# Compact 64x64 operands for the two heads of a pair, in two quarters of TensorE (RWKV core and attention)

## The chip, the cores and the metric

The kernel runs on one core of a Trainium2 chip. The metric is the device time of one execution in microseconds (us), the median of several runs.

## What is computed

Two layers of an encoder over 256 tokens of width 1024, in float32. Each layer has a token mixer with four groups (attention, bidirectional RWKV-7, pooling, gated convolution) and a channel mixer (dense in layer 0, eight experts in layer 1). The change touches the RWKV group (4 heads of 64, in two directions) and the attention group (4 heads of 64).

```python
def rwkv7_step(S, inp):
    r, w, k, v, a_vec, b_vec = inp
    sa = jnp.einsum('...ij,...j->...i', S, a_vec)
    S = S * w[..., None, :] + sa[..., :, None] * b_vec[..., None, :] + v[..., :, None] * k[..., None, :]
    return S, jnp.einsum('...ij,...j->...i', S, r)
...
    xs = (to_time(r), to_time(decay), to_time(k), to_time(v), to_time(-kk), to_time(kk * a))
    S0 = jnp.zeros((2, bsz, H, N, N), jnp.float32)
    _, ys = lax.scan(rwkv7_step, S0, xs)
    ys = jnp.moveaxis(ys, 0, 2)
    y = ys[0] + jnp.flip(ys[1], axis=1)
...
    y_a = neighbourhood_attention(za[..., :G], za[..., G:2 * G], za[..., 2 * G:], rpb)
    y_b = rwkv7_bidirectional(zr, lg, mu, w0, w2, a0, a2, k_k, k_a, r_k, lnx_w, lnx_b, g2)
    y_c = multiscale_pool(zp, pool_w, pool_scale)
    y_d = short_gated_conv(zc, conv_w)
    return jnp.concatenate([y_a, y_b, y_c, y_d], axis=-1) @ w_out
```

## The kernel before

The program runs `mixer(0)`, `ffn_layer(0)`, `mixer(1)` and `moe_layer(1)` one after the other. Weights come in chunks of 1 MB through a ring of three `raw` tiles on SyncE's queue (`raw_chunk`, L208); `chunk` splits each into two float32r parts, `whi` on ScalarE (L220) and `wlo` on VectorE (L221), and a projection is three matmuls per block (L173 to L175).

The RWKV scan is done in four chunks of 64 tokens per direction, for two heads at a time. `rw_prep(hp)` prepares the operands of pair `hp`; `rw_core(hp)` does the scan. A tile holds the channels of the two heads one above the other, head 0 in partitions 0 to 63 and head 1 in 64 to 127. So that one 128x128 matmul serves both heads, `bd4` and `put_bd` (L381, L387) lay each operand out as a block-diagonal 128x128 matrix per chunk, zeros in the off-diagonal blocks (names bdA, bdB, bdK, bdV). All 128x128 intermediates, `X`, `XT`, `nT`, `P1`, `Ub`, `Sb`, have that form and are 512 columns wide for four chunks.

The steps of a core, with `e` for the two directions and four chunks `c` each:

- `s1` (bdB with `ar`, 128 moving columns) and `s3` (bdA with bdB) start `X` and `nT` (L544 to L557).
- Five levels invert a triangular matrix: VectorE transposes `X` into `XT` (L563), `p1` multiplies `nT` and `X`, ScalarE copies the result to `P1` (L568), `p2` multiplies `XT` and `P1`, VectorE copies it into `X` under a mask (L574). Between levels stand `s2` (bdK with `ar`, L582 to L584) and the transposes `sk` of V, B and K (L593, L595).
- The recurrence over four chunks: `sV` with `ak`, `Sb` with bdA, a copy `tU` (L610), `X` with `tU`, a copy `Ub` (L612), then `sK` and `sB` products and the new state `Sb` (L623, L625).
- The outputs `y`: for each head a sum of up to six products of 128x64 stationary columns, in the column half of that head.

Every part of the mixer is a generator: "z" the projections for RWKV, "q" and "r" `rw_prep(0)` and `rw_prep(1)`, "0" and "1" the two cores, "a" attention, "p" pooling, "c" convolution, "f" fillers (chunks of the conditioning weights, a product and sum of 128x1024 on VectorE, L257), "g" a row, "o" the output projections (matmuls named ya). The string `ORDER[l]` says which part makes its next step; a scheduler then sets the order on each engine, so projections (z, ya) stand between the steps of the cores. `psum` has two rings of four banks; a core takes its banks from one of them (`bk`).

Attention computes the scores of two heads as two matmuls of 128 rows against the same `kt`, with a query tile `qz` whose other half is zero (L713), into one bank; the values `pv` are computed for 128 columns of which 64 are used.

## Time and profile before

| | us |
|---|---|
| median of 3 runs (lowest, highest) | 1547.24 (1546.98, 1551.23) |
| the profiled execution | 1546.37 |
| its span, first to last instruction | 1544.5 |
| TensorE busy | 1443.1 (93%) |
| VectorE busy | 645.8 (42%) |
| ScalarE busy | 435.5 (28%) |
| GpSimd busy | 24.9 (2%) |

Busy shares are means over stages with different limits, so the sections below go by stage and by start times. A float32 matmul appears as two records of TensorE. A record's duration is the latency of one; records are pipelined, and their pace is the distance between starts.

### The profile page before, as it was taken

To read this page: it belongs to the slowest core of one execution; us is meant where nothing else is said; L and a number is where in the kernel's file an instruction comes from. 1 tells how busy PE (TensorE), PEld (TensorE's weight loads), DVE (VectorE), ACT (ScalarE), POOL (GpSimd) and SP (SyncE) were. 2 spreads that over 40 slices of the span, in tenths; PEclk is the share of its full clock that TensorE was granted. 3 is DMA by queue.
4 is the path that set the end of the run, shared out by engine and by line. 5 is a ranking of instruction groups with operands and counts; after the bars stand their busy time and mean duration, and the time that the engine had idled before them with its cause. 6 is when DMAs were issued, how large, how long until landed. Compare 5 with 4: busy or idle time off the path is not lost. (4 is left out here: it accounts for less than half of the span.)

```text
span 1544.5 us, 28342 instructions
## 1 busy us (share of the span) xinstructions
PE 1443.1 (93%) x12174; PEld 875.5 (57%) x12174; DVE 645.8 (42%) x1194; ACT 435.5 (28%) x814; POOL 24.9 (2%) x91
## 2 busy tenths in 40 slices
PE   3999989999998999989889899999999999998885
PEld 2988979999997999963223233433433234332222
DVE  7799869977856777651010021020020110110202
ACT  4854645544437746350011000010010010000101
POOL 1001000000001001000000000000000000000000
PEclk9999999999999999999999999999999999999998
DMA  9556138987743411189999999999999999999995
GB/s 373 215 204 227 55 146 340 394 339 306 293 158 122 158 55 42 45 323 363 416 415 416 417 417 417 416 415 382 412 417 416 417 415 416 416 415 416 416 410 194
DMA packets 85253, 487.79 MB, mean 316 GB/s; under 512 B 9841, under 2 KB 10225, under 8 KB 40946
## 3 DMA queue, kind: packets, MB, share of 16 engines
q1 hardware_dynamic: 83522, 482.98, 78.3%
q10 hardware_dynamic: 1584, 2.68, 0.6%
q8 instruction: 113, 1.85, 0.5%
q14 instruction: 34, 0.28, 0.0%
HBM read 484.57 MB, written 1.05 MB: 314 GB/s over the span
## 5 line engine op out<-in xcount | busy, mean ns | idle before, releaser
L170 PE MATMUL u<-mw,xe 128*32 128x512 f32 (+1 forms) x3368 | 359.0, 537 | 20.1 <-DMA mw<-in_moe_dram 18.7
L1179 DVE TENSOR_TENSOR sg<-sg,u 128x256 f32<-128x256 f32 (+1 forms) x96 | 34.3, 380 | 650.6 <-ACT sg L1178 650.6
L170 PEld LDWEIGHTS u<-mw,xe 128*32 128x32 f32 x3368 | 114.5, 109 | 220.8 <-issue 160.4
L1178 ACT ACTIVATE sg<-u 128x256 f32<-128x256 f32 (+1 forms) x96 | 30.8, 355 | 666.0 <-PE u L170 656.5
L170 PE MATMUL y<-mw,sT 128*32 128x512 f32 x1480 | 180.4, 594 | 15.5 <-DMA mw<-in_moe_dram 10.8
L221 DVE TENSOR_TENSOR wlo<-raw,whi 128x1024 fp32r<-128x1024 f32 x142 | 169.8, 1218 | 46.7 <-ACT whi L220 46.5
L220 ACT ACTIVATE whi<-raw 128x1024 fp32r<-128x1024 f32 x142 | 146.4, 1056 | 137.1 <-issue 43.6
L170 PE MATMUL u<-mwhi,xe 128*32 128x512 f32 (+1 forms) x748 | 172.6, 551 | 0.4 <-PEq L1132 0.3
L170 PE MATMUL u<-mwlo,xe 128*32 128x512 f32 (+1 forms) x748 | 150.7, 551 | 0.5 <-PEq L1132 0.2
L174 PE MATMUL g<-hlo,whi 128*128 128x256 f32 x448 | 126.9, 284 | 0.5 <-DVE hlo L339 0.3
L173 PE MATMUL g<-hhi,whi 128*128 128x256 f32 x448 | 126.9, 284 | 0.0
L175 PE MATMUL g<-hhi,wlo 128*128 128x256 f32 x448 | 126.6, 283 | 0.0
L170 PEld LDWEIGHTS y<-mw,sT 128*32 128x32 f32 x1480 | 52.5, 109 | 128.0 <-issue 84.7
L257 DVE CUSTOM_DVE_ANT_0 raw<-raw,row,pcs 128x1024 f32<-128x1024 f32 x96 | 120.3, 1278 | 4.5 <-ACT row L1362 3.9
L170 PE MATMUL y<-mwhi,sT 128*32 128x512 f32 x324 | 96.2, 594 | 0.1
L173 PE MATMUL z<-hhi,whi 128*128 128x256 f32 x304 | 88.9, 293 | 4.1 <-ACT whi L220 4.0
L170 PEld LDWEIGHTS u<-mwhi,xe 128*32 128x32 f32 x748 | 46.2, 109 | 79.7 <-issue 70.0
L175 PE MATMUL z<-hhi,wlo 128*128 128x256 f32 x304 | 88.1, 290 | 2.2 <-DVE wlo L221 2.2
L174 PE MATMUL z<-hlo,whi 128*128 128x256 f32 x304 | 87.6, 289 | 0.5 <-DVE hlo L339 0.3
L174 PEld LDWEIGHTS g<-hlo,whi 128*128 128x128 f32 x448 | 85.9, 192 | 1.6 <-DVE hlo L339 1.2
L173 PEld LDWEIGHTS g<-hhi,whi 128*128 128x128 f32 x448 | 86.0, 192 | 0.6
L175 PEld LDWEIGHTS g<-hhi,wlo 128*128 128x128 f32 x448 | 85.9, 192 | 0.0
(317 smaller groups left out, 2022.8 us busy)
## 6 DMA issues: line engine op xcount, KB each, us to landing
mw<-in_moe_dram SPq DMA_DIRECT2D x232, 1024.0 KB, 15.0
mwlo<-in_moe_dram SPq DMA_DIRECT2D x104, 512.0 KB, 12.6
mwhi<-in_moe_dram SPq DMA_DIRECT2D x104, 512.0 KB, 13.8
raw<-in_ada_dram SPq DMA_DIRECT2D x44, 1024.0 KB, 6.7
raw<-in_ffn_dram SPq DMA_DIRECT2D x42, 1024.0 KB, 7.1
raw<-in_win_dram SPq DMA_DIRECT2D x20, 1024.0 KB, 4.9
raw<-in_wout_dram SPq DMA_DIRECT2D x6, 1024.0 KB, 5.0
raw<-in_ada_dram SPq DMA_DIRECT2D x8, 512.0 KB, 7.1
```

What stands on the lines that cost most here:

```text
L170: pe.matmul(o, a, b, start=start, stop=stop)
L173: pe.matmul(o, ah, bh, start=start, stop=False)
L174: pe.matmul(o, ah, bl, start=False, stop=False)
L175: pe.matmul(o, al, bh, start=False, stop=stop)
L220: ops[0].append(act.activation(hi, raw[:, c], AF.Copy))
L221: ops[1].append(dve.tensor_sub(lo, raw[:, c], hi.bitcast(F32)))
L257: r = dve.tensor_tensor_reduce(w, w, cB, scale=1.0, scalar=P(l, "ab", v * KB + k), op0=OP.mult, op1=OP.add, accum_out=mods[l][:, v, k:k + 1])
L1178: other_set(act.activation(sg, u[:, 0:w], AF.Silu))
L1179: dve.tensor_mul(sg, sg, u[:, w:2 * w])
```

## The change

Block-diagonal operands are gone. `mmh` makes each product as two 64x64 matmuls, one per head: rows 0 to 63 into partitions 0 to 63 of the bank, rows 64 to 127 into partitions 64 to 127. Every tile of the core that was 512 columns wide for four chunks becomes 256 wide (`half`, a ring of 38; the wide ring goes from 47 to 36), and masks, `tU` and `sd` are half as wide. `rw_prep` hands `bc`, `kf`, `zv` and `ar` on as they are, without the 16 copies and 16 fills per pair. The transposes `sk` become products with a 64x64 identity. `y` alternates the heads product by product. In attention the query tile is compact, each head's scores are a matmul over 64 rows into a bank of its own, two additions of 256 columns take the place of one of 512, and `pv` computes 64 columns. The first half of the last output projection becomes a part of its own, "O", behind the other parts; `ORDER` is unchanged.

```diff
...
-NSLOT = 47
+NSLOT = 36
+NHALF = 38
...
-            def bd4(name):
-                b = slot_(name).rearrange("p (n h t) -> p n h t", n=4, h=2)
-                pool.memset(b[0:64, :, 1, :], 0.0)
-                pool.memset(b[64:128, :, 0, :], 0.0)
-                return b
-
-            def flat(b, n):
-                return b[:, n].rearrange("p h t -> p (h t)")
+            def half(name):
+                return mp.tile([128, 256], F32, name=name, tag="h", bufs=NHALF).rearrange("p (n f) -> p n f", n=4)
 
             HS = [slice(0, 64), slice(64, 128)]
 
-            def put_bd(b, src):
-                for h in range(2):
-                    act.activation(b[HS[h], :, h, :], src[HS[h]], AF.Copy)
+            def mmh(o, a, b, start=True, stop=True):
+
+                for h in HS:
+                    mm(o[h], a[h], b[h], start, stop)
...
                 zv = zmix(4 + hp, "zdv")
-                B = {n: [] for n in "ABKV"}
-                for e in range(2):
-                    for n, src in (("B", c4(bc)[:, e]), ("A", ar[e][:, :, 0, :]), ("K", c4(kf)[:, e]),
-                                   ("V", c4(zv)[:, e])):
-                        b = bd4("bd" + n)
-                        put_bd(b, src)
-                        B[n].append(b)
-                    yield
-                st_r[hp] = dict(eP=eP, ar=ar, bc=c4(bc), B=B)
+                st_r[hp] = dict(eP=eP, ar=ar, B=c4(bc), K=c4(kf), V=c4(zv))
+                yield
...
                 for e in range(2):
-                    X[e] = v4(slot_("X"))
-                    act.activation(X[e], ident[:, None, :].to_broadcast([128, 4, 128]), AF.Copy)
+                    X[e] = half("X")
+                    act.activation(X[e], b4(C("i2")[:, None, :]), AF.Copy)
                     p = bk[hp]("s1").rearrange("p (c m t) -> p c m t", c=4, m=2)
                     for c in range(4):
-                        mm(p[:, c], flat(B["B"][e], c), ar[e][:, c])
-                    dve.copy_predicated(X[e].rearrange("p n (h t) -> p n h t", h=2),
-                                        b4(mx[:, 0, e].rearrange("p (h t) -> p h t", h=2)[:, None]),
-                                        p[:, :, 0:1, :].to_broadcast([128, 4, 2, 64]))
+                        mmh(p[:, c], R["B"][:, e, c], ar[e][:, c])
+                    dve.copy_predicated(X[e], b4(mx[:, 0, e, None, :]), p[:, :, 0, :])
                     dve.tensor_mul(arb[:, 4 * e:4 * e + 4, :], p[:, :, 1, :], b4(m1i[:, e, None, :]))
-                    p = v4(bk[hp]("s3"))
+                    p = pq("s3")
                     for c in range(4):
-                        mm(p[:, c], flat(B["A"][e], c), flat(B["B"][e], c))
-                    nT[e] = v4(slot_("nT"))
+                        mmh(p[:, c], ar[e][:, c, 0], R["B"][:, e, c])
+                    nT[e] = half("nT")
                     dve.tensor_mul(nT[e], p, b4(m3[:, e, None, :]))
-                    XT[e] = v4(slot_("XT"))
+                    XT[e] = half("XT")
...
                 for lv in range(NLV):
-                    pt = [None, None]
                     P1 = [None, None]
                     for e in range(2):
                         dve.transpose(XT[e], X[e])
-                        pt[e] = v4(bk[hp]("p1"))
+                        p = pq("p1")
                         for c in range(4):
-                            mm(pt[e][:, c], nT[e][:, c], X[e][:, c])
-                        P1[e] = v4(slot_("P1"))
-                        act.activation(P1[e], pt[e], AF.Copy)
+                            mmh(p[:, c], nT[e][:, c], X[e][:, c])
+                        P1[e] = half("P1")
+                        act.activation(P1[e], p, AF.Copy)
                         yield
                     for e in range(2):
-                        p = v4(bk[hp]("p2"))
+                        p = pq("p2")
                         for c in range(4):
-                            mm(p[:, c], XT[e][:, c], P1[e][:, c])
+                            mmh(p[:, c], XT[e][:, c], P1[e][:, c])
                         dve.copy_predicated(X[e], b4(mx[:, lv + 1, e, None, :]), p)
...
-                                mm(p[:, c], flat(B["K"][e], c), ar[e][:, c])
+                                mmh(p[:, c], R["K"][:, e, c], ar[e][:, c])
                             dve.tensor_mul(ark[:, 4 * e:4 * e + 4, :], p[:, :, 1, :], b4(m1i[:, e, None, :]))
-                            ak[e] = v4(slot_("ak"))
-                            dve.tensor_mul(ak[e].rearrange("p n (h t) -> p n h t", h=2),
-                                           p[:, :, 0:1, :].to_broadcast([128, 4, 2, 64]),
-                                           b4(m1s[:, e, None]))
+                            ak[e] = half("ak")
+                            dve.tensor_mul(ak[e], p[:, :, 0, :], b4(m1s[:, e, None]))
                             yield
                     elif lv <= 3:
                         nm = "VBK"[lv - 1]
                         for e in range(2):
-                            p = v4(bk[hp]("sk"))
+                            p = pq("sk")
                             for c in range(4):
-                                pe.transpose(p[:, c], flat(B[nm][e], c), ident)
-                            b = v4(slot_("s" + nm))
+                                mmh(p[:, c], R[nm][:, e, c], C("i2"))
+                            b = half("s" + nm)
                             act.activation(b, p, AF.Copy)
                             (sV, sB, sK)[lv - 1][e] = b
...
                         c = i if e == 0 else 3 - i
-                        pu = v4(bk[hp]("u"))
-                        mm(pu[:, 0], ak[e][:, c], sV[e][:, c], True, i == 0)
+                        pu = pq("u")
+                        mmh(pu[:, 0], ak[e][:, c], sV[e][:, c], True, i == 0)
                         if i:
-                            mm(pu[:, 0], flat(B["A"][e], c), Sb[e][:, c], False, True)
-                        t_ = mp.tile([128, 128], F32, name="tU", tag="tU", bufs=2)
+                            mmh(pu[:, 0], ar[e][:, c, 0], Sb[e][:, c], False, True)
+                        t_ = mp.tile([128, 64], F32, name="tU", tag="tU", bufs=4)
                         dve.tensor_copy(t_, pu[:, 0])
-                        mm(pu[:, 1], X[e][:, c], t_)
+                        mmh(pu[:, 1], X[e][:, c], t_)
                         dve.tensor_copy(Ub[e][:, c], pu[:, 1])
                         if i < 3:
                             tc_ = c * 64 + (63 if e == 0 else 0)
                             dec = R["eP"][:, e, tc_:tc_ + 1]
                             if i:
-                                sd = mp.tile([128, 128], F32, name="sd", tag="sd", bufs=2)
+                                sd = mp.tile([128, 64], F32, name="sd", tag="sd", bufs=4)
                                 act.activation(sd, Sb[e][:, c], AF.Copy, scale=dec)
-                            mm(pu[:, 2], sK[e][:, c], sV[e][:, c], True, False)
-                            mm(pu[:, 2], sB[e][:, c], Ub[e][:, c], False, True)
+                            mmh(pu[:, 2], sK[e][:, c], sV[e][:, c], True, False)
+                            mmh(pu[:, 2], sB[e][:, c], Ub[e][:, c], False, True)
...
-                    for h in range(2):
-                        for j, (a, b) in enumerate(seq):
-                            mm(yp[HS[h], c * 64:(c + 1) * 64], a[:, HS[h]], b, j == 0, j == len(seq) - 1)
+                    for j, (a, b) in enumerate(seq):
+                        mmh(yp[:, c * 64:(c + 1) * 64], a, b, j == 0, j == len(seq) - 1)
...
-                qz = []
-                for hp in range(2):
-                    q_ = et("qz")
-                    qz.append(q_)
-                    for h in range(2):
-                        pool.memset(q_[HS[1 - h], h, :], 0.0)
-                        act.activation(q_[HS[h], h, :], p[HS[h], hp, :], AF.Copy, scale=0.125)
+                qt = et("qt")
+                act.activation(qt, p, AF.Copy, scale=0.125)
...
-                        p = pa("sc").rearrange("p (h t) -> p h t", h=2)
+                        s = et("sc")
+                        ps = [pa("sc") for _ in range(2)]
                         for h in range(2):
-                            mm(p[:, h, :], qz[hp][:, h, qs], kt[:, hp, :])
-                        s = et("sc")
-                        dve.tensor_add(s, p, bi)
+                            mm(ps[h][:, 0:T], qt[HS[h], hp, qs], kt[HS[h], hp, :])
+                        for h in range(2):
+                            dve.tensor_add(s[:, h, :], ps[h][:, 0:T], bi[:, h, :])
...
-                                mm(po[:, i, :], pt[:, h, k, :], vn[:, k, hp * 128:(hp + 1) * 128], k == 0, k == 1)
+                                mm(po[:, i, HS[h]], pt[:, h, k, :], vn[:, k, hp * 128 + 64 * h:hp * 128 + 64 * h + 64],
+                                   k == 0, k == 1)
...
-                yield from out_proj(3, yrw, False, False, 0)
...
-                     "f": fill(99), "g": gate_row(), "r": rw_prep(1), "1": rw_core(1), "o": outs()}
-            needs = {"q": "z", "0": "q", "1": "r", "r": "z", "o": "apc0", "g": "f" if l == 0 else ""}
+                     "f": fill(99), "g": gate_row(), "r": rw_prep(1), "1": rw_core(1), "o": outs(),
+                     "O": out_proj(3, yrw, False, False, 0)}
+            needs = {"q": "z", "0": "q", "1": "r", "r": "z", "o": "apc0", "O": "0", "g": "f" if l == 0 else ""}
...
-            for k in ORDER[l] + "zq0apcfgr1o":
+            for k in ORDER[l] + "zq0apcfgro1O":
                 step(k)
-            for k in "zq0apcfgr1o":
+            for k in "zq0apcfgro1O":
...```

The order on the engines follows. First TensorE in the recurrence of the second core of layer 0, before (u are the products of the recurrence, ya_1670 to ya_1671 two banks of the output projection):

```order
L170 MATMUL p_1932<-P_1922,XT 128x128 x4
L170 MATMUL p_1938<-P_1930,XT 128x128 x4
L170 MATMUL u<-sV,ak 128x128 x3
L174 MATMUL ya_1670<-wlo,yhi 128x512
L170 MATMUL u<-sV,ak 128x128
L170 MATMUL u<-tU,X 128x128
L175 MATMUL ya_1670<-whi,ylo 128x512
L170 MATMUL u<-tU,X 128x128
L173 MATMUL ya_1671<-whi,yhi 128x512
L170 MATMUL u<-sV,sK 128x128
L170 MATMUL u<-Ub,sB 128x128
```

The same place in the change, where shapes 64x64 are one head's product:

```order
L167 MATMUL p_2134<-P_2120,XT 64x64 x8
L167 MATMUL p_2144<-P_2132,XT 64x64 x8
L167 MATMUL u<-sV,ak 64x64 x6
L170 MATMUL ya_1752<-whi,yhi 128x512
L167 MATMUL u<-sV,ak 64x64 x2
L171 MATMUL ya_1752<-wlo,yhi 128x512
L167 MATMUL u<-tU,X 64x64 x4
L172 MATMUL ya_1752<-whi,ylo 128x512
L170 MATMUL ya_1753<-whi,yhi 128x512
L167 MATMUL u<-sV,sK 64x64 x2
L167 MATMUL u<-Ub,sB 64x64 x2
```

Four products of the level and each product of the recurrence are now twice as many rows, and projections still stand between them, so 64-row and 128-row matmuls alternate. Over the whole program runs of matmuls of 64 stationary columns between wider ones are 9 before (all in y) and, with the scores, 86 after: 24 and 15 in the two cores of layer 0, 28 and 19 in those of layer 1.

Second VectorE at the start of the first core of layer 0, before (ISA rows are the product and sum of a filler):

```order
L548 COPY_PREDICATED X<-mk,s_578 128x512
L551 TENSOR_TENSOR arb<-s_578,cs 128x256
L556 TENSOR_TENSOR nT<-s_585,cs 128x512
L221 TENSOR_TENSOR wlo<-raw,whi 128x1024
L548 COPY_PREDICATED X<-mk,s_595 128x512
L551 TENSOR_TENSOR arb<-s_595,cs 128x256
L556 TENSOR_TENSOR nT<-s_602,cs 128x512
L221 TENSOR_TENSOR wlo<-raw,whi 128x1024
L563 STREAM_TRANSPOSE XT<-X 128x512
```

And in the change:

```order
L537 COPY_PREDICATED X<-mk,s_563 128x256
L538 TENSOR_TENSOR arb<-s_563,cs 128x256
L543 TENSOR_TENSOR nT<-s_574,cs 128x256
L549 STREAM_TRANSPOSE XT<-X 128x256
L218 TENSOR_TENSOR wlo<-raw,whi 128x1024 x2
L549 STREAM_TRANSPOSE XT<-X 128x256
L254 ISA raw,mods_70<-raw,row_67,pcs_68 128x1024
```

The operations are the same in kind; those of the core are half as wide, and the splits and fillers stand a few places later among them.

## Rows read from the trace of the kernel before

**Rows 1.** Busy time by stage: stretch, length, PE, PEld, DVE, ACT, POOL, PEclk, DMA share, GB/s

```profile
60.00:160.00 100.00, 93.72 (x807) 89.30 (x806) 94.82 (x183) 57.58 (x118) 5.03 (x18) 1.00 0.55 197
160.00:211.00 51.00, 49.58 (x443) 46.58 (x441) 36.35 (x72) 22.66 (x41) 0.00 (x0) 1.00 0.19 63
...
231.00:470.00 239.00, 237.57 (x1679) 223.84 (x1680) 189.19 (x257) 107.59 (x125) 0.00 (x0) 0.99 0.77 301
...
500.00:592.00 92.00, 90.95 (x739) 87.74 (x738) 69.53 (x125) 58.86 (x115) 5.33 (x18) 1.00 0.27 93
592.00:657.00 65.00, 64.74 (x608) 61.01 (x606) 44.07 (x85) 30.45 (x57) 0.00 (x0) 1.00 0.17 55
...
700.00:1520.00 820.00, 783.31 (x7175) 272.60 (x7166) 103.58 (x248) 57.77 (x147) 0.00 (x0) 1.00 1.01 413
```

**Rows 2.** Groups of TensorE, whole span: line, operation, tiles, records, busy us, mean ns, idle

```profile
L170 PE MATMUL p<-X,nT 128*128 128x128 f32 x320 | 40.7, 276 | 1.7 <-DVE nT L556 1.5
...
L170 PE MATMUL y<-ark,sV 128*64 128x64 f32 x128 | 14.4, 234 | 0.0
...
L170 PE MATMUL s<-ar,bdB 128*128 128x128 f32 x64 | 8.9, 280 | 1.5 <-issue 1.4
```

**Rows 3.** Timeline of TensorE, recurrence of the fourth core: start us, us, operation, records

```profile
643.10 0.38 PE L170 MATMUL u<-sV,ak 128*128 128x128 f32 x2
643.32 0.39 PE L170 MATMUL u<-sV,sK 128*128 128x128 f32 x2
...
643.99 0.39 PE L170 MATMUL u<-sV,ak 128*128 128x128 f32 x2
```

**Rows 4.** Timeline of TensorE, the y sums of the fourth core, two heads

```profile
652.79 0.33 PE L170 MATMUL y<-ark,sV 128*64 128x64 f32 x2
...
653.19 0.28 PE L170 MATMUL y<-ark,sV 128*64 128x64 f32 x2
653.31 0.22 PE L170 MATMUL y<-arb,Ub 128*64 128x64 f32 x1
653.31 0.27 PE L170 MATMUL y<-ark,sV 128*64 128x64 f32 x1
653.36 0.22 PE L170 MATMUL y<-arb,Ub 128*64 128x64 f32 x1
...
656.60 0.28 PE L170 MATMUL y<-arb,Ub 128*64 128x64 f32 x2
```

**Rows 5.** Timeline of TensorE: whole height (ya), column groups (u), row groups (cb)

```profile
225.00 0.40 PE L174 MATMUL ya<-wlo,yhi 128*128 128x512 f32 x1
225.24 0.39 PE L175 MATMUL ya<-whi,ylo 128*128 128x512 f32 x1
...
802.46 1.92 PE L170 MATMUL u<-mw,xe 128*32 128x512 f32 x16
804.31 1.66 PE L170 MATMUL cb<-yhl,oT 64*128 64x512 f32 x11
```

**Rows 6.** Timeline of TensorE, 128- and 64-column products in turn, second core

```profile
205.35 0.39 PE L170 MATMUL u<-sV,ak 128*128 128x128 f32 x2
205.67 0.33 PE L170 MATMUL y<-ark,sV 128*64 128x64 f32 x2
...
206.25 0.39 PE L170 MATMUL u<-tU,X 128*128 128x128 f32 x2
```

**Rows 7.** Groups of VectorE by shape, whole span

```profile
L1181 DVE STREAM_TRANSPOSE sT<-sg 128x256 f32<-128x256 f32 x72 | 29.0, 429 | 0.8
L574 DVE COPY_PREDICATED X<-mk,p 128x512 f32<-128x512 uint8 x40 | 28.8, 726 | 15.9 <-PE p L170 15.8
L563 DVE STREAM_TRANSPOSE XT<-X 128x512 f32<-128x512 f32 x40 | 27.4, 698 | 0.4
```

**Rows 8.** Groups of ScalarE, whole span

```profile
L568 ACT ACTIVATE P<-p 128x512 f32<-128x512 f32 x40 | 23.7, 596 | 21.3 <-PE p L170 21.3
...
L387 ACT ACTIVATE bdV<-zdv 64x256 f32<-64x256 f32 x16 | 6.7, 416 | 0.2
```

## What the change will do to the time: a prediction

> **What bounds the kernel now.** I read the table of stages first [rows 1]. The program is two token mixers, the dense channel mixer between them (231 to 470 us), and the expert channel mixer behind them (from 700 us in the table). In the expert stage the 16 DMA engines are fully busy (share 1.01, 413 GB/s) and in the dense one TensorE is (237.6 of 239.0 us); the change has no instruction in either. Both begin when the mixer ahead of them gives its buffers free, so what a mixer loses or gains reaches the end one to one. What is left is four RWKV cores, one per pair of heads and layer: 60 to 160, 160 to 211, 500 to 592 and 592 to 657 us. There TensorE is busy 94, 97, 99 and 99.6% [rows 1]. Busy could still mean latency only, so I looked at starts: matmul records of 128x128 by 128 follow one another every 0.111 us (643.10 to 643.99 us holds eight) [rows 3] although one takes 276 ns [rows 2]. They are issued at a fixed pace, so in the last three stretches TensorE's issue is the bound. In the first, VectorE is busy 94.8 of 100 us as well, and it is the tighter of the two.
>
> **The paces.** An f32 matmul shows as two records. A 128x128 matmul with 128 moving columns costs 2 x 0.111 = 0.222 us [rows 3]. Records with 64 stationary columns and 64 moving ones follow every 0.058 us (0.12 for two) [rows 4]. Can two small ones run at once? In the same group the second head's column half begins at 653.31, in the same moment as the first half's next record: two streams run beside each other, into one PSUM bank, and each keeps 0.058. The trace has two more cases [rows 5]: sixteen records of four column groups take 1.92 us, that is four in about 0.43; and the half-height matmuls of two row groups (cb, two different banks) do 11 records in 1.66 us, about 0.13 each behind the first's latency, where full-height records (ya) of the same 512 columns start 0.24 apart. No row has tiles that differ in both row and column group and share a bank, which is what the change issues. The two ends for a pair of heads are therefore 2 x 0.058 = 0.117 us (side by side) and 4 x 0.058 = 0.233 us (one behind the other), against 0.222 before. I take 0.117, since column groups in one bank and row groups in two banks both overlap in the rows.
>
> **What TensorE loses.** Per core, s3 has 8 matmuls, the five levels 80 and the recurrence 34, together 122. At 0.222 each these are 27.1 us, at 0.117 they are 14.2: 12.9 us less. The y sums are 88 records in 3.9 us now (86 from 652.79 to 656.60, partly overlapped) [rows 4], then 44 pairs of records at 0.058 = 2.6 us: 1.3 less. s1 and s2 keep 128 moving columns, so two heads side by side take what one block-diagonal matmul took (nothing, or +0.22 each without overlap). The 24 transposes per core, one record each at the same pace (0.11), become pairs of 0.117: nothing. Sum per core 14.2, four cores 57 us. The attention scores, 8 matmuls per layer with 256 moving columns, halve: at twice the 128-column pace (0.22 per record) 1.7 us per layer. The pv matmuls keep their 128-column weights; I count nothing.
>
> **What TensorE pays.** Going from full to small matmuls and back costs time. From 205.35 to 206.25 us two full records, two small ones and two full ones run [rows 6]: by pace 4 x 0.111 + 2 x 0.058 = 0.56 us, by the trace 0.90. A round trip thus costs 0.34 us. In the order before there are 9 such runs of small matmuls, in the order of the change 86, because z and output projections stand between the steps of a core: 20 more in the first core, then 12, 27 and 18. By this price they are 6.8, 4.1, 9.2 and 6.1 us, 26 in all. The other end is nothing, where a run would have waited for its operand anyway.
>
> **VectorE and ScalarE.** The core's tiles have half the columns. A 512-wide predicated copy takes 726 ns and a transpose 698; a 256-wide transpose takes 429 [rows 7]. That is 0.27 us for 256 columns, and I take it for every operation of this kind: 10 predicated copies, 10 transposes and 6 masks per core lose 0.27 each, the 22 small ones of the recurrence, 64 columns less, 0.07: 8.5 us per core. Scores add 0.16 four times per layer (two 256-wide additions at 0.43 for one 512-wide at 0.70): 0.6. On ScalarE the 64 copies into block-diagonal tiles of 0.416 us go, 26.6 us, and the P copies of 596 ns shrink [rows 8]; GpSimd's fills go too. ScalarE bounds no stretch; only what stands between a prepared operand and the first s1 of a core (a few copies in the first layer) can show, and I give that 2 us in all.
>
> **The sum.** First core: TensorE -14.2 - 1.7 + 6.8 = -9.1, VectorE -8.5 + 0.6 = -7.9; the smaller counts, -8. Second: -14.2 + 4.1 = -10.1. Third: -14.2 - 1.7 + 9.2 = -6.7. Fourth: -14.2 + 6.1 = -8.1. In the last three the loop of a level (matmul, copy, matmul, predicated copy) becomes shorter on every engine, but less so than the matmuls, so some waits will open that TensorE's work covers now; I take nine tenths: -9.1, -6.0, -7.3. With the 2 us for ScalarE the sum is -32.4. The profiled execution took 1546.37 us (span 1544.5), 0.9 below the median; 1546.4 - 32.4 = 1514, and since part of the round trips will fall on waits for operands, I say 1510 (a sixth of their 26 us).
>
> **Rivals.** *The quadrants do not overlap* (slower). Both heads write one PSUM bank, from two row groups, and cb, the only row-group case in the trace, uses two banks [rows 5]. Then a pair costs 0.233 for 0.222 (488 pairs, +5 us), y becomes 88 records in a row (4 x 1.2 = +5), s1 and s2 double (64 x 0.22 = +14), the transposes double (96 x 0.12 = +12), and the 26 us of round trips stay: +62 on TensorE, of which VectorE's relief and the 6 idle us of the first stretch take back some 10, so about 1598. Between a pair at 0.117 (-61 + 26 = -35 on TensorE) and one at 0.233 (+62) the sign turns near 0.16 us a pair; from there it decides. Against it speak the y halves, which overlap inside one bank. The Trainium skill (TensorEngine Tiling (Array Packing), Gotcha 1: PSUM Pressure) says that different row tiles cannot access the same PSUM bank at the same time; by that rule this rival is the forecast. The rows neither bear it out nor refute it, so I leave it 10 in 100.
>
> *The loops become the bound* (smaller gain). If each core is held by its chain through ScalarE and VectorE, about half of the 32 us stays: 1530. For it: VectorE is busy 69.5 of 92 us in the third stretch and its share rises when the stretch shrinks. Against it: in the second and fourth it is busy 36 of 51 and 44 of 65 [rows 1].
>
> *The round trips cost nothing* (larger gain). If they fall on waits, the last three stretches lose 14.2, 15.9 and 14.2, the first stays with VectorE: 0.9 x 44 + 8 + 2 = 50, so 1496.
>
> *The cores do not matter.* If something else held the mixers (the load of weights), the time would stay within 1542 to 1551. The DMA share there is 0.17 to 0.55 [rows 1], which speaks against it.
>
> **How the numbers follow.** Forecast with its own range 1500 to 1521: 50 in 100. Larger gain, below 1500: 20, of which about 8 below 1490. Smaller gain, 1521 to 1542: 15. No change, within 0.3% (what a measurement of this kernel tells from none): 5. Slower, the first rival: 10. From 1490 to 1541 leaves out 8 below and some 15 above, near two in ten. Faster is 50 + 20 + 15 = 85, same 5, slower 10.
>
> **What the profile of the changed kernel will show.** If the pace is right, the records of p and u of a level start 0.03 us apart on average, and the 16 matmuls of a level, 3.6 us by pace now, are through in about 1.9 us of issue. If the first rival holds, they start 0.058 apart. Round trips show as a gap of 0.09 us and more ahead of each weight load that changes the size. If VectorE holds the first stretch, it is still above 90% busy there. The expert stage must look as before, only earlier; if it does not begin earlier by what the mixers lost, the step from mixer to end is wrong.

## The result and the profile after

The changed kernel takes 1521.66 us (median of four runs, 1518.97 to 1523.92); the kernel before took 1547.11 beside it (1546.45 to 1551.23). The ratio is 0.9829, with a 95% interval of 0.9806 to 0.9853: 25.5 us less. The forecast was 1510, the range 1490 to 1541. The profiled execution of the changed kernel took 1518.97 us (span 1517.2) and is the fastest of its four, so the traces below show 27.4 us less (1546.37 to 1518.97).

The stages of the changed kernel, in the columns of [rows 1] (stretch, length, busy time of PE, PEld, DVE, ACT and POOL with counts, granted clock, DMA share, GB/s):

```profile
60.00:155.00 95.00, 87.44 (x1146) 78.15 (x1145) 83.39 (x182) 42.70 (x90) 0.14 (x2) 0.95 0.52 184
155.00:200.00 45.00, 41.89 (x787) 34.75 (x787) 31.22 (x77) 14.89 (x31) 0.00 (x0) 0.96 0.32 111
...
220.00:459.00 239.00, 238.11 (x1678) 224.69 (x1679) 189.24 (x257) 107.93 (x125) 0.00 (x0) 0.99 0.77 301
489.00:575.00 86.00, 84.60 (x1074) 75.68 (x1073) 60.38 (x129) 47.94 (x95) 0.14 (x2) 1.00 0.29 99
575.00:631.00 56.00, 55.85 (x967) 45.77 (x965) 34.77 (x85) 19.65 (x39) 0.52 (x1) 1.00 0.17 58
674.00:1494.00 820.00, 777.01 (x7154) 273.55 (x7170) 103.70 (x248) 57.84 (x147) 0.00 (x0) 1.00 1.01 413
```

The dense and the expert stage are as before, only earlier. In layer 1 TensorE is still busy 98 and 99.7%. In layer 0 it is not: 92 and 93%, and there the granted clock is no longer 1.00. When the stages begin and end, from the first or last instruction of the tile named, says where the time went (us from the start of the span):

| | before | after | change of this stage |
|---|---|---|---|
| end of the first core, layer 0 (last y) | 148.0 | 142.5 | -5.5 |
| end of the second core, layer 0 (last y) | 211.1 | 200.5 | -5.1 |
| dense stage begins (first ht) | 231.1 | 220.3 | -0.2; mixer of layer 0 in all -10.8 |
| mixer of layer 1 begins (first ht) | 481.9 | 471.0 | -0.1 |
| end of the third core (last y) | 600.4 | 582.6 | -6.9 |
| end of the fourth core (last y) | 656.9 | 631.1 | -8.0 |
| expert stage begins (first gx) | 682.4 | 656.6 | 0; mixer of layer 1 in all -14.9 |
| end of the span | 1544.5 | 1517.2 | -1.5 |

The prediction had -8, -9.1, -6.0 and -7.3 for the four cores and -2 for ScalarE. (The times are rounded; a sum of them can be off by 0.1.) Layer 1 gave a little more than that, layer 0 well over a third less. The last row's 1.5 us is no part of the change: from gx to the end the kernels below take 861.5 to 863.7 us, the kernel before 862.1, the changed one 860.6.

The operations became as short as expected. Groups of the changed kernel, in the columns of [rows 2, 7, 8]:

```profile
L167 PE MATMUL p<-X,nT 64*64 64x64 f32 x640 | 24.8, 220 | 0.6 <-ACT sB L579 0.4 <-DVE X L560 0.2
...
L560 DVE COPY_PREDICATED X<-mk,p 128x256 f32<-128x256 uint8 x40 | 17.5, 438 | 16.4 <-PE p L167 16.3
L549 DVE STREAM_TRANSPOSE XT<-X 128x256 f32<-128x256 f32 x40 | 16.7, 432 | 0.4
...
L554 ACT ACTIVATE P<-p 128x256 f32<-128x256 f32 x40 | 15.1, 384 | 16.4 <-PE p L167 14.9
```

A masked copy went from 726 to 438 ns, a transpose from 698 to 432, the P copy from 596 to 384.

What is new are waits in layer 0. The timeline of TensorE there (start us, us, operation, records, idle before and who ended it):

```profile
83.10 1.92 PE L167 MATMUL s<-ar,kf 64*64 64x128 f32 x32
84.85 1.10 PE L167 MATMUL p<-X,nT 64*64 64x64 f32 x32
89.49 0.93 PE L731 MATMUL pT<-cs,sc 128*128 128x128 f32 x4 [3.54 <-ACT sc L725]
```

Thirty-two records of small products take 1.10 us, the latency of the last one (0.22) included: starts 0.03 us apart, as the prediction asked for when quarters run beside each other. The 32 records of s ahead of them (eight pairs with 128 moving columns) take 1.75 us from start to start, 0.22 per pair: what one block-diagonal product took, as the prediction had it. Behind the p records TensorE stands still for 3.5 us. Its row names ScalarE's sc, but that waits for VectorE, and VectorE waits for the attention bias (bi), which a DMA brings. The waits of VectorE from 60 to 155 us (who waits, for whom: us in all, times, longest):

```profile
DVE sc L721 <- DMA bi<-in_rpb_dram: 4.4, 2, 2.2
```

and of TensorE from 60 to 220 us:

```profile
PE pT L731 <- ACT sc L725: 3.5, 1, 3.5
PE s L167 <- DVE yrw L645: 2.8, 1, 2.8
PE u L167 <- DVE Sb L608: 1.6, 1, 1.6
```

In the kernel before VectorE waited for bi once, for 1.1 us, and TensorE never for yrw. Where the second core of layer 0 lost its part is seen when the time from the first core's last y to its own is cut in two, ten microseconds behind its first s1 (160.1 us before, 155.7 after). Before, then after, in the columns above:

```profile
148.00:170.00 22.00, 20.58 (x153) 19.32 (x153) 19.38 (x40) 17.08 (x36) 0.00 (x0) 1.00 0.27 96
170.00:211.00 41.00, 41.00 (x386) 39.05 (x384) 28.18 (x55) 14.39 (x25) 0.00 (x0) 1.00 0.16 52
```

```profile
142.50:165.70 23.20, 20.39 (x178) 18.67 (x179) 23.20 (x47) 10.39 (x19) 0.00 (x0) 0.93 0.56 194
165.70:200.50 34.80, 34.51 (x717) 28.80 (x716) 20.52 (x56) 11.15 (x25) 0.00 (x0) 1.00 0.20 70
```

The second part became 6.2 us shorter, and TensorE is busy through all of it. The first became 1.2 us longer; VectorE was busy for 19.4 of its 22 us before and is for all of it (23.2) after.

Behind TensorE's pauses the granted clock falls. Windows of the changed kernel, ahead of a fall, in it and behind it, in the columns above:

```profile
84.00:90.60 6.60, 2.82 (x56) 2.21 (x52) 4.35 (x7) 1.24 (x5) 0.00 (x0) 1.00 0.46 187
90.60:97.40 6.80, 6.30 (x49) 5.19 (x50) 4.69 (x12) 1.00 (x3) 0.00 (x0) 0.50 0.95 320
97.40:104.00 6.60, 6.60 (x78) 6.40 (x79) 5.31 (x13) 2.18 (x7) 0.00 (x0) 1.00 0.32 117
120.00:124.70 4.70, 2.72 (x47) 1.90 (x46) 4.08 (x11) 1.35 (x5) 0.00 (x0) 1.00 0.69 237
124.70:128.20 3.50, 3.50 (x27) 3.16 (x27) 2.76 (x11) 2.37 (x8) 0.00 (x0) 0.51 0.57 178
...
158.00:162.30 4.30, 1.49 (x10) 0.87 (x8) 4.30 (x10) 1.16 (x3) 0.00 (x0) 1.00 0.43 181
162.30:165.70 3.40, 3.40 (x19) 2.79 (x19) 3.40 (x8) 1.23 (x2) 0.00 (x0) 0.50 0.72 239
```

Three times TensorE stands still for a good part of a stretch (it is busy for 2.82 of 6.6, 2.72 of 4.7 and 1.49 of 4.3 us), and then works at 0.50, the lower of its two levels (1.2 GHz), for 6.8, 3.5 and 3.4 us. What that costs shows in products of one kind: the ya records of this trace start 0.24 us apart where the clock is whole (161.51, 161.75, 161.98) and 0.43 apart in the last of these stretches (164.16, 164.59, 165.01). In the kernel before the clock is 1.00 over both cores of layer 0 [rows 1].

### The profile page after: what moved, and what is told of

Read it like the earlier page. It is cut to its first block, busy times and chain, and to the rows that moved or that the text cites. A ratio compares the mean times of both kernels' runs of the same rounds, so it can differ in the third digit from the quotient of the medians.

```text
span 1517.2 us, 30871 instructions
## 1 busy us (share of the span) xinstructions
PE 1407.0 (93%) x13541; PEld 826.1 (54%) x13566; DVE 611.6 (40%) x1202; ACT 392.4 (26%) x744; POOL 1.9 (0%) x19
## 5 line engine op out<-in xcount | busy, mean ns | idle before, releaser
L167 PE MATMUL u<-mw,xe 128*32 128x512 f32 (+1 forms) x3368 | 358.7, 537 | 22.5 <-DMA mw<-in_moe_dram 18.3
L167 PEld LDWEIGHTS u<-mw,xe 128*32 128x32 f32 x3368 | 115.0, 109 | 219.1 <-issue 159.6
L167 PE MATMUL y<-mw,sT 128*32 128x512 f32 x1480 | 180.7, 594 | 17.1 <-DMA mw<-in_moe_dram 12.7
L218 DVE TENSOR_TENSOR wlo<-raw,whi 128x1024 fp32r<-128x1024 f32 x142 | 170.3, 1220 | 53.1 <-ACT whi L217 51.3
L217 ACT ACTIVATE whi<-raw 128x1024 fp32r<-128x1024 f32 x142 | 147.0, 1058 | 146.4 <-issue 47.6
L167 PE MATMUL u<-mwhi,xe 128*32 128x512 f32 (+1 forms) x748 | 172.4, 551 | 1.2 <-issue 0.5
L167 PE MATMUL u<-mwlo,xe 128*32 128x512 f32 (+1 forms) x748 | 150.9, 551 | 1.9 <-issue 1.2
L171 PE MATMUL g<-hlo,whi 128*128 128x256 f32 x448 | 127.2, 284 | 0.1
L170 PE MATMUL g<-hhi,whi 128*128 128x256 f32 x448 | 127.3, 284 | 0.0
L172 PE MATMUL g<-hhi,wlo 128*128 128x256 f32 x448 | 127.0, 284 | 0.0
L167 PEld LDWEIGHTS y<-mw,sT 128*32 128x32 f32 x1480 | 52.9, 109 | 128.3 <-issue 84.9
L254 DVE CUSTOM_DVE_ANT_0 raw<-raw,row,pcs 128x1024 f32<-128x1024 f32 x96 | 120.3, 1279 | 4.2 <-ACT row L1341 3.8
L167 PE MATMUL y<-mwhi,sT 128*32 128x512 f32 x324 | 95.9, 594 | 0.0
L170 PE MATMUL z<-hhi,whi 128*128 128x256 f32 x304 | 89.2, 294 | 4.8 <-ACT whi L217 4.1
L167 PEld LDWEIGHTS u<-mwhi,xe 128*32 128x32 f32 x748 | 46.3, 109 | 80.3 <-issue 71.0
L172 PE MATMUL z<-hhi,wlo 128*128 128x256 f32 x304 | 87.7, 288 | 2.3 <-DVE wlo L218 2.3
L171 PE MATMUL z<-hlo,whi 128*128 128x256 f32 x304 | 88.2, 291 | 0.5 <-DVE hlo L336 0.3
L170 PEld LDWEIGHTS g<-hhi,whi 128*128 128x128 f32 x448 | 86.5, 193 | 0.6
L171 PEld LDWEIGHTS g<-hlo,whi 128*128 128x128 f32 x448 | 86.3, 193 | 0.8 <-DVE hlo L336 0.4
L172 PEld LDWEIGHTS g<-hhi,wlo 128*128 128x128 f32 x448 | 86.3, 193 | 0.0
## 6 DMA issues: line engine op xcount, KB each, us to landing
mw<-in_moe_dram SPq DMA_DIRECT2D x232, 1024.0 KB, 15.1
```

The costliest lines, as they stand in the source:

```text
L167: pe.matmul(o, a, b, start=start, stop=stop)
L170: pe.matmul(o, ah, bh, start=start, stop=False)
L171: pe.matmul(o, ah, bl, start=False, stop=False)
L172: pe.matmul(o, al, bh, start=False, stop=stop)
L217: ops[0].append(act.activation(hi, raw[:, c], AF.Copy))
L218: ops[1].append(dve.tensor_sub(lo, raw[:, c], hi.bitcast(F32)))
```

## The experiments

**Do the two quarters run at the same time?** Two of the three kernels on this question add products that nothing reads; they leave nothing of the computation out. The first only changes the order in a burst, that is, in the eight products of four chunks and two heads that go into one bank (p1 is shown; s1, s3, p2, s2 and sk have the same edit):

```diff
+            def mm4(f):
+                for h in HS:
+                    for c in range(4):
+                        o, a, b = f(c)
+                        mm(o[h], a[h], b[h])
...
-                        for c in range(4):
-                            mmh(p[:, c], nT[e][:, c], X[e][:, c])
+                        mm4(lambda c: (p[:, c], nT[e][:, c], X[e][:, c]))
...
```

> Kernel of the change, but in each burst of four chunks (s1, s3, p1, p2, s2, sk) all four products of head 0 are issued, then all four of head 1; the recurrence and y keep the heads side by side. Nothing is left out. Theory (two quarters run at the same time, in one bank, and TensorE's issue is the bound): a burst of sixteen records that takes 4 x 0.117 = 0.47 us side by side takes 0.93 in a row, 28 bursts per core; the four bursts with 128 moving columns go from about 0.85 to 1.7. Per core 28 x 0.46 + 4 x 0.85 = 16.3, four cores 65; nine tenths of that on the path, 59: about 1580 (1570 to 1590). Rival (the loops through ScalarE and VectorE are the bound, TensorE has room): less than half of it, 1521 to 1545. Rival (the quarters do not really overlap, the gain came from elsewhere): no change, 1520 to 1524.

Measured: 1539.64 us (ratio to before 0.9947, 0.993 to 0.9964), 18 more than the change, where the theory had 59. The timeline tells why, here in the first core of layer 1:

```profile
549.48 1.54 PE L167 MATMUL p<-X,nT 64*64 64x64 f32 x32
550.91 1.36 PE L167 MATMUL p<-P,XT 64*64 64x64 f32 x29
552.06 0.27 PE L167 MATMUL sk<-cs,zdv 64*64 64x64 f32 x1
552.12 0.22 PE L167 MATMUL p<-P,XT 64*64 64x64 f32 x1
552.17 0.22 PE L167 MATMUL sk<-cs,zdv 64*64 64x64 f32 x1
...
```

Records of p2 and of the next burst, sk, alternate: while head 1's half of one burst runs in its quarter, head 0's half of the next burst runs in the other. The experiment did not take the overlap away; it left it within a run of bursts, and each run pays one half-burst more, 4 x 0.117 = 0.47 us (two bursts 1.43 us from start to start here, three halves). The 21 us by which gx came later would be 45 such runs; this is an estimate, the runs were not counted. By the size of the result alone one would have chosen the wrong rival, that TensorE has room; the next two runs correct that. In both edits `pf` is the whole bank of which `p` is the first half, and what is shown for p1 stands in p2 as well. First two pairs, one product per head each:

```diff
...
+                            if c == 1:
+                                for _ in range(2):
+                                    mmh(pf[:, 256:320], C("i2"), C("i2"))
...
```

> As the run with a full product inside each burst, but with two pairs of small products (64x64 identity times itself, both heads, two columns blocks of the same bank that nothing reads) in its place: 80 x 2 x 0.117 = 18.7 us by pace, without a change of size. Theory (TensorE's issue is the bound): 1539 (1532 to 1542), some 25 us below the run with the full product. Rival (the loops are the bound and TensorE has room): 1522 to 1530.

Then the same four products in head 0's quarter:

```diff
...
+                            if c == 1:
+                                for _ in range(4):
+                                    mm(pf[0:64, 256:320], C("i2")[0:64], C("i2")[0:64])
...
```

> As the run with two pairs of small products inside each burst of p1 and p2 (18.6 us more than the change for 80 times four products of 64x64), but all four in head 0's quarter, one behind another. Theory (each quarter has a stream of its own at 0.117 us per product, and four products in one take as long as four pairs): 80 x 4 x 0.117 = 37 us: 1559 (1554 to 1561). Rival (TensorE hands out products at a fixed pace, whatever their quarter): as with the pairs, 1540.

Measured: 1540.30 us with two pairs, 18.6 more than the change (0.233 for each of the 80), and 1557.33 with the same four products in one quarter, 35.7 more (0.446 each). The bursts, with the pairs and then in one quarter:

```profile
548.29 0.40 PE L167 MATMUL p<-cs 64*64 64x64 f32 x8
548.52 0.63 PE L167 MATMUL p<-X,nT 64*64 64x64 f32 x16
548.99 0.40 PE L167 MATMUL p<-cs 64*64 64x64 f32 x8
```

```profile
541.49 0.57 PE L167 MATMUL p<-cs 64*64 64x64 f32 x7
...
541.90 0.22 PE L167 MATMUL p<-cs 64*64 64x64 f32 x1
541.95 0.40 PE L167 MATMUL p<-X,nT 64*64 64x64 f32 x7
```

Eight records in two quarters take 0.23 us from start to start (548.29 to 548.52), in one quarter 0.46 (541.49 to 541.95). Both write one bank. So each quarter has a stream of its own at 0.117 us per product. That both kernels pay nearly the whole of it also says that TensorE's issue, not the loops, sets the time of the cores, above all in layer 1 (+9.8 by the pairs, where the pace gives 9.3).

**What does a round trip cost?**

```diff
...
+                            if c == 1:
+                                mm(pf[:, 256:384], ident, ident)
...
```

> Kernel of the change with one more product in every burst of p1 and p2 (80 in all), between its second and third chunk: a 128x128 identity times itself, into columns of the same bank that nothing reads. Theory (going from small products to a full one and back costs 0.34 us, and TensorE's issue is the bound): 80 x (0.222 + 0.34) = 45 us: 1567 (1555 to 1572). Rival (round trips cost nothing beyond the pace): 80 x 0.222 = 18: 1539 (1532 to 1542), the same as with small products in that place.

Measured: 1557.0 us, 35.3 more than the change, 0.44 for each of the 80; between the theory (45) and the rival (18). The timeline has the price:

```profile
553.48 0.49 PE L167 MATMUL p<-cs 128*128 128x128 f32 x2
553.90 0.68 PE L167 MATMUL p<-X,nT 64*64 64x64 f32 x16
554.51 0.49 PE L167 MATMUL p<-cs 128*128 128x128 f32 x2
```

From one full product to the next it takes 1.03 us. The full one is 0.222 and the four small pairs between are 0.47 by pace, so 0.34 are left, exactly the price that the prediction read from [rows 6]: 0.20 on the way to the small ones, 0.14 on the way back. But it is paid in full only where TensorE never waits. From ht to gx layer 1 takes 21.2 us longer for 40 insertions, which is 0.31 beyond the full product's 0.222. From ht to ht layer 0 takes only 11.2 us longer, 0.06 beyond it (its first ht itself comes 2.2 us later in this trace, ahead of any insertion). In layer 0 the insertions filled pauses: the wait ahead of pT is gone, that for yrw is 1.3 instead of 2.8 us, and the half clock nearly goes. Both cores of layer 0 in this kernel:

```profile
62.00:157.00 95.00, 92.14 (x1156) 79.61 (x1155) 82.35 (x179) 42.44 (x89) 0.14 (x2) 0.98 0.58 204
157.00:215.00 58.00, 56.74 (x875) 46.10 (x874) 33.85 (x81) 17.59 (x37) 0.00 (x0) 1.00 0.17 56
```

The clock is 0.98 and 1.00, where the change has 0.95 and 0.96. The Trainium skill (TensorEngine Tiling (Array Packing), Key Properties) says that changing the tiling mode drains TensorE. The rows agree in so far as a change of size costs time, and give it the price; what it consists of they do not show.

**Why did layer 0 fall short?** First the wait for the bias:

```diff
...
             def attention():
+                bis = {}
+                for qb in range(2):
+                    for hp in range(2):
+                        bis[qb, hp] = et("bi")
+                        act.dma_start(bis[qb, hp], rpb[l, qb, hp])
                 p = z_pair(3, pa)
...
-                        bi = et("bi")
-                        act.dma_start(bi, rpb[l, qb, hp])
+                        bi = bis[qb, hp]
```

> Kernel of the change, but the four loads of the attention bias (bi) of each layer are issued at the start of attention instead of one step ahead of their use. Theory (the first core of layer 0 lost a part of its gain because VectorE stands still for bi twice, 2.25 and 2.11 us, with the core's transposes behind it in its queue, and TensorE, standing still for 3.5 us, is then granted half its clock for 6.8 us): both waits and the half clock behind 90 us go; the half clock costs about half of what TensorE does in it, 3 us, and the waits 2 to 4: 1521.7 - 5 = 1516.5 (1514 to 1519), with the first core's y about 5 us earlier than 142.3. Rival (VectorE's own work holds the first core, the wait for bi only takes time that it would wait anyway): first core unchanged within 1 us, time 1520 to 1523. Rival (the half clock comes whatever TensorE did before): waits gone, half clock still there at about the same time, gain 2 us or less.

Measured: 1520.06 us (0.9825, 0.9808 to 0.9841), which can't be told from the change itself. Yet the first core ends 8.0 us earlier (134.5 for 142.5), more than the theory had. The waits of TensorE and two windows of this kernel:

```profile
PE s L167 <- DVE yrw L645: 7.7, 1, 7.7
```

```profile
60.00:131.00 71.00, 69.23 (x965) 60.94 (x965) 64.83 (x143) 34.07 (x73) 0.14 (x2) 1.00 0.53 195
147.00:193.00 46.00, 38.21 (x683) 31.23 (x680) 32.29 (x74) 16.88 (x33) 0.00 (x0) 0.89 0.35 128
```

The waits for bi and the half clock in the first core are gone (1.00, where the change has 0.93 over the same 71 us), but the second core now waits 7.7 us for yrw, where it waited 2.8, and has less of its clock. Of the 8.0 us the mixer of layer 0 keeps 3.3; and with the loads moved in layer 1 too, its mixer takes 1.9 us longer (187.5 from ht to gx for 185.6). What yrw stands behind, in VectorE's timeline of this kernel:

```profile
147.65 0.69 DVE L804 TENSOR_TENSOR cpr<-z,cc 128x512 f32<-128x512 f32 x1
148.26 1.28 DVE L254 CUSTOM_DVE_ANT_0 raw<-raw,row,pcs 128x1024 f32<-128x1024 f32 x1
...
149.46 1.67 DVE L811 SCALAR_TENSOR_TENSOR cy<-cpr,pcs,cy 128x256 f32<-128x256 f32 x4
151.05 1.28 DVE L254 CUSTOM_DVE_ANT_0 raw<-raw,row,pcs 128x1024 f32<-128x1024 f32 x1
...
156.45 0.41 DVE L645 TENSOR_TENSOR yrw<-yb,bo 128x256 f32<-128x256 f32 x1
```

The first core's last bank is free only after yrw, and the second core's fourth burst (its second s3, tile s) needs it. Ahead of it in the queue stand fillers (1.28 us each) and the convolution (cpr, cy). So the next kernel also moves yrw ahead of them, and moves bi in layer 0 alone (the kernel after that makes the same two edits in the kernel before):

```diff
-ORDER = (('00zzzzqqqaqaq0a00a0a0a00000pp00a000a00000pa00f000a00af00000a0000rcarf00rfrffccrcfffffo11gf'
+ORDER = (('00zzzzqqqaqaq0a00a0a0a00000pp00a000a00000pa00f000a00af00000a0000rcarf00rfr0ffccrcfffffo11gf'
...
+                if l == 0:
+                    for qb in range(2):
+                        for hp in range(2):
+                            load_bi(qb, hp)
```

> Kernel of the change with two edits in layer 0 alone: the four bias loads (bi) at the start of attention, as in the run before, and the last step of the first core (yrw, which frees the bank that the second core's fourth scores wait for) one place earlier in ORDER, ahead of two fillers and the convolution. With bi alone the first core's y ended at 134.5 instead of 142.5 us, but TensorE then waited 7.7 instead of 2.8 us for yrw, which stands in VectorE's queue behind fillers, cy and wlo. Theory (layer 0's missing gain is these waits and the half clock behind them, one after the other): the wait for yrw goes, the stretch behind it keeps its full clock, the mixer of layer 0 ends 4 to 6 us earlier than with bi alone, layer 1 is as in the change: 1513.5 (1511 to 1516). Rival (VectorE's work between the cores, busy without a gap from 131 to 163 us, is the bound itself): the wait moves on to another of its results, 1518 to 1521.

> Kernel before the change, with the same two edits in layer 0 (bias loads at the start of attention, yrw one place earlier). Its trace has one wait of VectorE for bi of 1.1 us and none of TensorE for yrw, and TensorE stands still for 6 us in its first core. Theory (the waits were uncovered by the shorter products): little, 0 to 3 us less, 1545.5 (1544 to 1548). Rival (the waits cost as much before, and the change has nothing to do with them): some 8 us less, 1539.

Measured: on the changed kernel 1519.71 us (1514.03 to 1521.09; 0.9824, 0.9808 to 0.9841), on the kernel before 1546.38 (0.9991, 0.9981 to 1.0002). The times of the first scatter, and its profiled execution is its fastest (1514.03). In that trace the mixer of layer 0 ends 6.5 us earlier than in the change (ht at 213.8 for 220.3), 17.3 earlier than before: in sum the 17.1 that the prediction had for its two cores, but not core by core, since by the ends of y (134.9 and 195.5) the first gained 13.1 and the second 2.5. On the kernel before the same two edits give 1.0 us at ht. So most of the waits belong to the change: shorter products uncovered them. But the median lies in the rival's range, not in the theory's, and the waits moved on. TensorE's next ones in the first of these kernels:

```profile
PE ya L170 <- ACT yhi L237: 3.2, 1, 3.2
PE ya L171 <- DVE wlo L218: 1.1, 1, 1.1
```

ScalarE's yhi stands behind a whi that waits 8.8 us for the load of the output projection (wout):

```profile
ACT whi L217 <- DMA raw<-in_wout_dram: 12.1, 2, 8.8
```

Three kernels follow this chain. X early: the identity copies of X are made in rw_prep, on top of the two edits before.

```diff
+                X0 = []
+                for e in range(2):
+                    X0.append(half("X"))
+                    act.activation(X0[e], C("i2")[:, None, :].to_broadcast([128, 4, 64]), AF.Copy)
...
-                    X[e] = half("X")
-                    act.activation(X[e], b4(C("i2")[:, None, :]), AF.Copy)
+                    X[e] = R["X0"][e]
```

> As the run with bi and yrw early, and the identity copies that start X (ScalarE) made at the end of rw_prep instead of the core's first step, where they stood behind two whi splits that wait for a DMA. Theory (X's copy is next in line at the start of a core): 1 to 2 us less than without it, 1512. Rival (the core's start waits for VectorE, not for X): the same within 1 us.

Then ORDER[0] on top of that, with the first projection later (eight letters, six of them steps of the second core; the lines taken out are those of the change):

```diff
-ORDER = (('00zzzzqqqaqaq0a00a0a0a00000pp00a000a00000pa00f000a00af00000a0000rcarf00rfr0ffccrcfffffo11gf'
-          '11101111111111111111111111111111111o1o1111foffoooooooofffffffffffffffff'),
+ORDER = (('00zzzzqqqaqaq0a00a0a0a00000pp00a000a00000pa00f000a00af00000a0000rcarf00rfr0ffccrcfffff11gf'
+          '1111o1111111111111111111111111111111o1o1111foffoooooooofffffffffffffffff'),
```

> As the run with bi, yrw and X early, and the first output projection (o) of layer 0 placed five steps later in ORDER, behind the row bc and the first p1 products of the second core. In that run TensorE stood still for 3.2 and 1.1 us in front of ya, whose weights (wout) came late, had half its clock for 3.2 us behind it, and the core's first p1 products stood behind ya in its queue. Theory (the second core of layer 0 is held by projections queued ahead of its own products whose weights are late): those waits are filled by p1, p2 and their copies, the half clock there goes, the mixer of layer 0 ends 4 to 6 us earlier, 1511 (1508 to 1513). Rival (the load of the weights sets the end of this mixer, in whatever order TensorE works): the wait moves behind the core, 1515 to 1518.

Or, in its place, with the five fillers between the cores spread over the second core (the lines taken out are the same two):

```diff
+ORDER = (('00zzzzqqqaqaq0a00a0a0a00000pp00a000a00000pa00f000a00af00000a0000rcarf00rfr0ffccrco11gf'
+          '111011f1111f1111f1111f1111f1111111111111o1o1111foffoooooooofffffffffffffffff'),
```

> As the run with bi, yrw and X early, and the five fillers that ORDER of layer 0 has in a row between the two cores (each a load of 1 MB and two passes of 1.28 us on VectorE) spread over the levels of the second core. Without this edit VectorE is busy without a gap from 131 to 163 us, the weights of the first output projection (wout) come behind the fillers' loads in SyncE's queue, and TensorE stands still there for 4.3 us and has half its clock for 3.2. Theory (the second core of layer 0 starts late because of VectorE's fillers and their loads, not because of its own products): VectorE's row of work ends some 10 us earlier, the wait for yhi goes, the clock stays full, the mixer of layer 0 ends 4 to 6 us earlier than at 213.1: 1511.5 (1508 to 1513). Rival (the fillers take as much from the second core as they gave it between the cores, through its transposes and masked copies): the same within 2 us, 1514.5 to 1518.5.

Measured: 1516.31 us (0.9805, 0.9788 to 0.9822), 1516.36 (0.9796, 0.9779 to 0.9812) and 1514.43 (0.9777, 0.9756 to 0.9798). In the traces the mixer of layer 0 ends at 213.1, 213.8 and 213.2 us in all three: X early leaves TensorE's waits as they were (3.3 and 1.1 us for yhi and wlo), and its lower median is not told apart from that of the run before it; the other two remove the wait that they were meant for, and the time is given back at the next one. With the projection later, then with the fillers later (the wait of TensorE, and the window of the second core's y sums):

```profile
PE bc L167 <- DVE arb L541: 5.3, 1, 5.3
```

```profile
PE u L167 <- DVE Sb L609: 1.7, 1, 1.7
```

```profile
189.20:195.30 6.10, 6.10 (x112) 5.96 (x110) 1.50 (x6) 0.00 (x0) 0.00 (x0) 0.52 0.65 270
```

In the first, a bank that VectorE has not yet emptied (arb) takes the place of the late weights. In the last, the long wait is gone and the second core reaches its y sums at 189.2 us instead of 191.3, but VectorE, which now has the fillers inside the core, is waited for at the recurrence (as in the change, where it was 1.6 us), and the y sums run at a mean clock of 0.52: 6.1 us for 3.5. By their traces the rivals stand in both. The last kernel's median is the lowest of all, and its interval lies below that of the change, but not below those of the other two; its five times are 1511.57 to 1518.64, and the profiled one (1515.23) is none of its fastest, so its trace does not say where it gains.

**How much does VectorE hold?** The transposes and masked copies of its levels are done twice:

```diff
...
                         dve.transpose(XT[e], X[e])
+                        dve.transpose(XT[e], X[e])
...
                         dve.copy_predicated(X[e], b4(mx[:, lv + 1, e, None, :]), p)
+                        dve.copy_predicated(X[e], b4(mx[:, lv + 1, e, None, :]), p)
```

> Kernel of the change, but VectorE does each transpose of X into XT and each masked copy into X of the five levels twice (20 more per core, 0.34 us apart when queued, 6.8 us per core: about the 8.5 us that the half-width operations save). Theory (VectorE holds the first core; TensorE's issue the others, where only the chain of a level gets longer): first core +6, the others +1 to +2 each: 1532 (1528 to 1537). Rival (VectorE's relief is most of the gain in every core): +6 to +8 in each: 1549 (1545 to 1554).

Measured: 1538.3 us (0.9937, 0.9913 to 0.996), 16.6 more, between the two. By the ends of y the four cores lost 3.4, 9.6, 3.9 and 1.1 us. The theory put the loss into the first core; it is in the second, which now begins behind this wait:

```profile
PE s L167 <- DVE yrw L647: 10.3, 1, 10.3
```

So it is VectorE's queue between the two cores of layer 0 that has no room: 7.5 us of the second core's loss are this wait. The first core hides half of the 6.8 us that were added to it, layer 1 two thirds. In layer 0 nothing of the gain is left: its mixer ends at 231.7 us, with the kernel before at 231.1. There the gain rests on VectorE's shorter operations too, and not on the shorter products alone; layer 1 loses 5.0 of its 14.9 us.

**Attention.** The three edits in attention() undone (query tiles qz, scores into one bank, values of 128 columns; the scores are shown):

```diff
...
+                            mm(p[:, h, :], qz[hp][:, h, qs], kt[:, hp, :])
-                            mm(ps[h][:, 0:T], qt[HS[h], hp, qs], kt[HS[h], hp, :])
...
```

> Kernel of the change with the attention of before: query tiles with a zero half, scores over 128 rows into one bank with one addition of 512 columns, values of 128 columns; the core is that of the change. Theory (scores at twice the pace save 1.7 us per layer, values nothing, two additions cost VectorE 0.6): 1521.7 + 1.5 to 3.5: 1524. Rival (attention stands beside the cores, and its part of the change does nothing that shows, or costs some round trips of its own): within 1 us of 1521.7, or up to 2 below.

Measured: 1523.37 us (1521.54 to 1529.56; 0.9848, 0.9825 to 0.9871). Its interval overlaps that of the change, and in the traces gx begins at 656.4 us, with the change at 656.6; the mixer of layer 0 is 1.4 shorter and that of layer 1 1.2 longer. What attention's part is worth is not settled; it is small.

## Why the forecast held, and where it was off

The measured 1521.66 us lie in the stated range, but 0.7 us above the forecast's own (1500 to 1521), at the edge of the branch of a smaller gain, which had 15 in 100.

- **What bounds.** Right. The expert stage began 25.8 us earlier, which is what the mixers lost, and its own length stayed.
- **The pace of a pair.** Right: 0.117 us, by the pairs (0.233 for two) and by one quarter (0.446 for four). The first rival, 0.233 for a pair in one bank, falls, and with it the use that the prediction made of the rule of the Trainium skill (TensorEngine Tiling (Array Packing), Gotcha 1: PSUM Pressure), that different row tiles cannot access one PSUM bank at the same time. Here the two tiles write the two halves of the partitions of one bank, and the measurement decides: they do, and at full pace. Another page of the Trainium skill (PSUM — Partial Sum Buffer, section PSUM bank collisions raise a hardware error) quotes the same rule, but reports collisions of row tiles only within one bank and one quadrant (32 partitions), and none between quadrants of a bank for pairs of different engines; that part spoke against the rival. No run here shows a collision.
- **The round trips.** The price, 0.34 us, is right, as the insertions show. What share falls on waits was wrong. The prediction subtracted a sixth of the 26 us. By the insertions about a tenth is hidden in layer 1 (0.31 of 0.34 shows) and most of it in layer 0 (0.06 shows), where pauses and half clock took it up. At these rates 32 round trips in layer 0 and 45 in layer 1 make 2 + 14 = 16 us; this is a rough estimate, since the insertions stand inside bursts and the round trips of the change elsewhere. The rival by which they cost nothing falls with the 0.31.
- **Layer 1.** Right within 1 us per core: -6.9 and -8.0, forecast -6.0 and -7.3. TensorE's whole relief, -6.7 and -8.1, would have been nearer: the tenth taken off for the loops was not needed.
- **Layer 0, first core.** Too much: -5.5 for -8. The step that failed is "the smaller counts, -8". It compared TensorE's and VectorE's sums of work and left out waits for a transfer. When the core runs faster the bias loads, issued one step ahead, come too late (4.4 us), VectorE has the core's transposes behind that wait, and TensorE loses its clock for 6.8 us. With the loads early the core ends 8.0 us sooner still, 13.5 in all. Of these 1.4 came ahead of its first s1, and 2.4 came on the kernel before from the run with bi and yrw early; the 9.7 that are left are near TensorE's own 9.1 and above VectorE's 7.9 (an estimate: the parts are taken to add up). So that VectorE "is the tighter of the two" in this stretch does not hold: it is busy 88% after, under the 90% that the prediction set as its sign.
- **Layer 0, second core.** Too much: -5.1 for -9.1. The step that failed is "in the last three stretches TensorE's issue is the bound". It holds inside this core (34.5 of 34.8 us), not at its start. VectorE's queue between the two cores (preparation, fillers, convolution, the first core's end) did not become shorter with the products, it is busy for 23.2 of 23.2 us there, and the second core's levels begin behind it. The prediction had read VectorE's 36 of 51 us there and took a mean over the stretch for room at its start. The rival "the loops become the bound" asked for half the gain everywhere; what came is a full gain in layer 1 and three fifths of it in layer 0, not through the loops but through a queue and a transfer. That the queue holds the second core's start rests on VectorE's full row and on the run with its work done twice; no run shortens that row. In the traces with yrw, X, the weights or the fillers moved, the second core still takes 60.6 to 61.1 us from the first core's last y, where it took 58.0 in the change and 63.1 before: what the first core gained there was in part lost in the second.
- **ScalarE.** Too much by about half: the first s1 came 1.5 us earlier in layer 0 (they are part of the first core's 5.5) and in layer 1, counted from ht, 0.4 later, where -2 was given.
- **Attention.** Not settled.
- **The sum.** The cores were to give 30.4 us and ScalarE 2; the mixers gave 25.7 in all, 10.8 in layer 0 and 14.9 in layer 1. The 4 us more by which the forecast of 1510 lies below the sum's 1514 were the wrong correction: in layer 1 round trips are paid nearly in full, and in layer 0 other waits opened. The profile's own tests came out as written for the pace and the expert stage; the test for the first stretch (VectorE above 90%) was the first to say that something else holds it.

What stays open: how much the half clock costs by itself. No run removes it without also removing the pause ahead of it; its stretches in layer 0 add up to 13.7 us at half speed, so it is at most some 7. What would give the second core of layer 0 its missing 4 us: each wait that was removed came back elsewhere. And why the executions of the changed kernels scatter by 2 to 8 us: their mean clock follows it only in part (1514.03 us at 0.989 and 1519.96 at 0.988 with bi and yrw early).

## What to carry to other kernels

Two 64x64 products with their operands and results in opposite halves of the partitions took the time of one here (0.117 us), in one bank too; count them by quarters, and add 0.34 us for every round trip between full and small matmuls that no wait hides. When a stage becomes faster, list what was timed by its old length, loads issued just ahead of their use and other work in the queues between its parts, and price those from the queue's order and not from a busy share. And look at the stages one by one: here the kernel's time alone said "as forecast, a little less", while one layer gave all of it and the other three fifths.

## What was not expected of the hardware

Quarters overlap across bursts: with head 0's products all ahead of head 1's, the second half of a burst ran beside the first half of the next, and the order cost 18 us instead of 59. And the granted clock fell to 0.50 for 3.4 to 6.8 us behind stretches in which TensorE stood still for a good part (busy for 2.82 of 6.6, 2.72 of 4.7 and 1.49 of 4.3 us); ya records then start 0.43 us apart instead of 0.24, so that here a pause cost more than its own length.
